# Four more projection units as seven products, and the solve's transfers on two queues

## The chip, the cores and the metric

The kernel runs on one core of a Trainium2 chip. The metric is device time in microseconds of one execution; lower is better. A profiled execution gives a trace beside it: every instruction with its engine and time, every DMA, and who waited for whom. The engines are TensorE (PE, its weight loads PEld), VectorE (DVE), ScalarE (ACT), GpSimd (POOL) and SyncE (SP, which only issues DMAs here).

## The reference

One pre-norm residual layer over 1024 tokens of width 1024. Of one normalised input, a projection of 8208 columns feeds two mixers that run side by side: dilated attention in three groups, and a gated DeltaNet with a short causal convolution. Both are gated, projected up, merged by sigmoid gates and projected out. Cut to what matters here:

```python
h = _rmsnorm(x, norm_w[layer])
proj = h @ w_in[layer]
dsa_qkv, dsa_z, gdn_qkv, gdn_z, gdn_b, gdn_a, gate_a, gate_b = _split_columns(proj)
o_a = _dilated_mixture(q_a, k_a, v_a)
y_a = (o_a * jax.nn.silu(dsa_z)) @ w_up_a[layer]
cqkv = jax.nn.silu(_causal_depthwise_conv(gdn_qkv, conv_w[layer]))     # 4 taps
o_b = _gated_delta_rule(gq, gk, gv, g, beta)
y_b = (_rmsnorm(o_b, gdn_norm_w[layer]) * jax.nn.silu(gdn_z)) @ w_up_b[layer]
merged = jax.nn.sigmoid(gate_a) * y_a + jax.nn.sigmoid(gate_b) * y_b
x = x + merged @ w_out[layer]
# in _gated_delta_rule, per head and chunk of 64 tokens:
a = (k_beta @ k.T) * decay_strict
t_inv = triangular_solve(eye + a, eye)
u = t_inv @ (vc * beta)
w = t_inv @ (k_beta * jnp.exp(G))
# then a scan over the 16 chunks with a state per head
```

The result is (1, 1024, 1024) in float32.

## The kernel before, in words

**Products.** Inputs are float32; each operand is split into a high and a low float16 part, and a product is three float16 matmuls (lines L184 to L186 in `mm3_steps`). The normalised input stays in SBUF as `h_hi` and `h_lo`. The projection is cut into units of 256 columns: 18 for attention, 6 for the convolution (`gdn`, for two half-batches of heads `hb` and the kinds query 0, key 1, value 2), 4 for the output gates `z`, 8 for the merge gates (`gate`). A unit is done in one of two ways:

- `Normal`: four blocks of 128 columns by 512 tokens, each over 8 slices of the width, three matmuls a slice: 32 steps (ticks) of three matmuls. The weights come in two loads and are split in two calls of `split` (lines L167 for ACT, then L84 for DVE, 1024 elements each).
- `Seven`: a 2x2 by 2x2 block product with seven products instead of eight (a Strassen form). 7 x 4 ticks of three matmuls. Sums of the input's blocks (`sums`) are made once; sums of the weights' blocks are made on DVE (L329), and seven blocks of 512 are split (L330 on ACT, L84 on DVE). `seven_products` uses the three PSUM banks `ps_mm` in turn, copies between them on ACT (L367), and hands out results in the order (column block, token half) = (0,0), (1,1), (1,0), (0,1); the second and third come with a `rest` from which DVE subtracts the bank.

**Order.** PE runs in the order in which the program is written. `feed` holds the units in a list; `feed.tick(n)` writes the next n ticks into PE's order, between the steps of attention, of the solve or of the scan, `feed.until(name)` writes ticks until that unit is done, and `feed.later(n, fn)` runs a step n ticks on. For the other engines `set_orders` at the program's end plans an order from costs; on the chip each engine works its order off strictly, and a semaphore holds it where an operand is not there.

**The place of the change** lies between the last attention set and the scan. For each half `hb`: `decay` makes `E` (tiles `gm`), `sumsq` turns the keys and sums squares (`kss`), `pairs` makes key products, and DVE multiplies them by `E` into `MT`. `keys_side` stores `MT`'s diagonal blocks to DRAM (`m_d`) in four DMAs; `solve` loads them back as `As`, 128 systems of 32x32, one a partition, and works 31 steps of two DVE instructions (`stmp`, `X`), then a last scaling, and stores `X` (`u_d`) and its negated transpose `T` (`t_d`). Four loads bring `u_d` back into `MT` (there called `U`), two bring `t_d` to `T1p`. `merge` joins the 32x32 blocks to 64x64: `left` on PE reads `T1p`, DVE makes `Y` of it, `right` on PE reads `Y` and `U`. Both solves run one behind the other on DVE, in shared buffers. `state_parts` then makes and stores `un_d` and `w_d` for the scan. The weight loads (`wstage`) are issued by POOL, as are the stores `un_d` and `a_d`; the rest here by SP.

**Convolution.** `conv_unit` takes each block from PSUM to `xc` (515 columns: three of the quarter before, then 512), scales the last tap on ACT into `ca`, and adds three taps on DVE (three instructions `ca<-xc,cw,ca`), then applies the SiLU. It needs the two token halves of a column block in order, since the second starts with the last three columns of the first.

Of the kernel before, what the change touches and what calls it, by code (L numbers as in the profile page):

```python
# [38 lines left out]
def gdn_unit(hb, what):  # L39
# [6 lines left out]
          + [U_GATE + i for i in (0, 1, 2, 6, 7)] + [U_Z + i for i in range(4)])  # L46
# [11 lines left out]
STATE_LAG = 12  # L58
# [20 lines left out]
def hybrid_block(ctx: ExitStack, tc: tile.TileContext, A):  # L79
# [916 lines left out]
    def conv_unit(hb, what, dst_of, then=None):  # L996

        def gen(w):
            for c in range(2):
# [3 lines left out]
                for hf in range(2):  # L1003
                    def take(p):
                        with tc.high_priority():
# [8 lines left out]
                            for j in (2, 1, 0):  # L1014
                                STT(a, xc[:, j:j + 512], cw[:, cidx, j:j + 1], a, ALU.mult, ALU.add)
                            parts = [(dst[:, 8 * hf:8 * hf + 8].rearrange("p c i -> p (c i)"), lambda x: x)]
                            if hb:

                                dv = dst[:, 8 * hf:8 * hf + 8].rearrange("p (t c) i -> p t c i", c=2)
                                parts = [(dv[:, :, b], lambda x, b=b: x.rearrange("p (t c i) -> p t c i", c=2, i=64)[:, :, 1 - b])  # L1020
                                         for b in range(2)]
                            if (hb, what) in SILU:
                                for d, of in parts:
                                    SC.activation(d, of(a), AF.Silu, scale=2.0)
                            else:
                                th = pre[0].tile([128, 512], F32, name="cth", tag="cth", bufs=2)
                                SC.activation(th, a, AF.Tanh)
                                for d, of in parts:
                                    STT(d, of(th), 1.0, of(a), ALU.add, ALU.mult)
# [6 lines left out]
        feed.add(("gdn", hb, what), Normal(A["w"][gdn_unit(hb, what)]), gen)  # L1036
# [145 lines left out]
    def decay(hb):  # L1182

        for t in range(8):
# [18 lines left out]
            feed.tick(2)  # L1203
# [23 lines left out]
    def sumsq(hb, src, dst, take=None):  # L1227

        for t0 in range(0, 8, 2):
# [11 lines left out]
            feed.tick(2)  # L1241
# [36 lines left out]
    def keys_side(hb):  # L1278
# [12 lines left out]
        for kb in range(4):  # L1291
            b = kb % 2
            nc.sync.dma_start(out=m_d[kb].rearrange("n j i -> j n i"),
                              in_=MT[hb][32 * kb:32 * kb + 32].rearrange("p t e q i -> p (t e q) i")[:, :, 32 * b:32 * b + 32])
# [13 lines left out]
    def solve(hb, m_d, bsc):  # L1308
# [24 lines left out]
        for kb in range(4):  # L1333
# [4 lines left out]
            nc.sync.dma_start(out=U[32 * kb:32 * kb + 32].rearrange("p t e q i -> p (t e q) i")[:, :, 32 * b:32 * b + 32],  # L1338
# [128 lines left out]
    gate_unit(5, gate_spill)  # L1467
# [52 lines left out]
    for i in (6, 7):  # L1520
        gate_unit(i, gate_spill)
# [851 lines left out]
```

## Time and profile before

| | |
|---|---|
| median of 3 runs | 1049.75 us (1048.6 to 1051.1) |
| profiled execution | 1048.82 us; its span in the trace 1047.0 us |
| PE busy | 1029.0 us, 98% |
| DVE busy | 885.7 us, 85% |
| ACT busy | 583.0 us, 56% |
| granted clock of TensorE | 0.998 |

Times in the trace count from the span's start. A group line gives the line of the code, the engine, what is written and read, count, busy time and mean length of one, and then the idle time of the engine just before it with what ended that wait. SPq rows are issues of DMAs, not their transfers.

### The profile page before, as it was taken

The page shows a single profiled execution, that of the slowest core. Times are in us where ns is not written, and L with a number is a line of the kernel's source. Part 1 is how long each engine was busy: PE and PEld are TensorE (multiplying, and loading weights), DVE is VectorE, ACT ScalarE, POOL GpSimd, SP SyncE. Part 2 cuts the span into 40 slices and gives each one's busy share as a digit, 9 for nine tenths or more (in the row PEclk, how much of TensorE's full clock was granted, in tenths as well). Part 3 has the DMA queues.
Part 4 walks back from the last instruction along what each step waited for, and adds up shares of the span by engine and source line. Part 5 has one row for each costly group of instructions (what it writes and reads, how often), then busy time and mean ns, then how long its engine had stood idle before and what let it go on. Part 6 is the DMA issues. An engine that isn't in the chain of part 4 may idle for free.

```text
span 1047.0 us, 24924 instructions
## 1 busy us (share of the span) xinstructions
PE 1029.0 (98%) x9962; PEld 632.9 (60%) x9962; DVE 885.7 (85%) x2052; ACT 583.0 (56%) x1322; POOL 56.1 (5%) x107
## 2 busy tenths in 40 slices
PE   6999999999999999999999999999999999999997
PEld 5995595775966855876655545545555555444444
DVE  6898988979979889989998897976588768899934
ACT  6455767777767766667756633344444345344523
POOL 0000000000000000010010000110100001000000
PEclk9999999999999999999999999999999999999999
DMA  8144531542624622470146357794874415743232
GB/s 284 64 129 114 138 112 62 152 112 78 186 84 116 165 91 74 118 201 28 43 161 183 113 134 202 258 278 150 266 254 152 142 62 176 288 124 117 67 115 81
DMA packets 99780, 148.53 MB, mean 142 GB/s; under 512 B 31168, under 2 KB 64704, under 8 KB 98512
## 3 DMA queue, kind: packets, MB, share of 16 engines
q1 hardware_dynamic: 69264, 84.64, 27.9%
q0 software_dynamic: 12320, 44.11, 13.4%
q10 hardware_dynamic: 18080, 18.20, 5.0%
q8 instruction: 78, 1.28, 0.5%
q14 instruction: 38, 0.31, 0.1%
HBM read 91.13 MB, written 36.90 MB: 122 GB/s over the span
## 4 chain that ended last, share of the span: by engine, by line
PE 84%; DVE 10%; ACT 2%; DMA 1%; issue 1%; SPq 0%; DVEq 0%; ACTq 0%
PE ps_mm L184 21%; PE ps_mm L186 20%; PE ps_mm L185 20%; PE ps_G L813 2%; PE ps_S L186 2%; PE ps_S L185 2%; PE ps_S L184 2%; DVE ca L84 1%; PE ps_S L790 1%; PE ps_S L792 1%; PE ps_G L185 1%; PE ps_G L186 1%; PE ps_G L184 1%; DVE sm L799 1%; DVE tl L87 1%
## 5 line engine op out<-in xcount | busy, mean ns | idle before, releaser
L186 PE MATMUL ps_mm<-h_hi,wlo 128*128 128x512 f16 (+1 forms) x504 | 189.3, 376 | 0.0
L184 PE MATMUL ps_mm<-h_hi,whi 128*128 128x512 f16 (+1 forms) x436 | 163.8, 376 | 0.0
L185 PE MATMUL ps_mm<-h_lo,whi 128*128 128x512 f16 (+1 forms) x436 | 163.5, 375 | 0.0
L186 PEld LDWEIGHTS <-wlo 128*128 128x128 f16 x748 | 73.2, 98 | 81.4
L184 PEld LDWEIGHTS <-whi 128*128 128x128 f16 x816 | 79.9, 98 | 65.7
L185 PEld LDWEIGHTS <-whi 128*128 128x128 f16 x816 | 79.9, 98 | 64.4
L803 ACT ACTIVATE sm<-sm,osb 128x128 f32<-128x128 f32 (+1 forms) x160 | 69.3, 434 | 34.9 <-DVE osb L799 33.3
L330 ACT ACTIVATE whi<-wstage 128x512 f16<-128x512 f32 x84 | 51.1, 626 | 30.0 <-DVE wstage L329 11.9
L799 DVE CUSTOM_DVE_ANT_0 sm<-ps_S,amask 128x128 f32<-128x128 f32 (+1 forms) x192 | 60.3, 345 | 6.6 <-PE ps_S L792 6.5
L87 DVE TENSOR_TENSOR tl<-ps_G,th 128x256 f16<-128x256 f32 (+1 forms) x96 | 51.7, 539 | 13.3 <-ACT th L818 13.0
L84 DVE SCALAR_TENSOR_TENSOR whi<-wstage,whi 128x512 f16<-128x512 f32 x84 | 57.2, 684 | 4.6 <-ACT whi L330 4.4
L329 DVE TENSOR_TENSOR wstage<-wstage 128x512 f32<-128x512 f32 x84 | 56.9, 685 | 0.8
L185 PE MATMUL ps_mm<-wlo,h_hi 128*128 128x256 f16 (+1 forms) x256 | 57.3, 246 | 0.0
L84 DVE SCALAR_TENSOR_TENSOR ca<-xc,cw,ca 128x512 f32<-128x512 f32 x72 | 53.7, 745 | 3.8 <-ACT ca L1013 3.3
L184 PE MATMUL ps_mm<-h_hi,wlo 128*128 128x512 f16 x136 | 51.6, 380 | 0.0
L185 PE MATMUL ps_mm<-h_lo,wlo 128*128 128x512 f16 x136 | 51.5, 379 | 0.0
L84 DVE SCALAR_TENSOR_TENSOR wlo<-wstage,whi 128x1024 f16<-128x1024 f32 x38 | 46.1, 1218 | 6.3 <-ACT whi L167 5.6
L818 ACT CAST th<-ps_G 128x256 f16<-128x256 f32 (+1 forms) x96 | 44.0, 458 | 12.5 <-PE ps_G L813 10.8
L813 PE MATMUL ps_G<-cons,sm 128*128 128x128 f32 x280 | 46.9, 274 | 1.3 <-ACT sm L803 1.2
L84 DVE SCALAR_TENSOR_TENSOR wlo<-wstage,wlo 128x512 f16<-128x512 f32 x63 | 42.4, 683 | 6.2 <-ACT wlo L330 6.2
L313 POOL DMA_DIRECT2D wstage<-in_w x42 | 22.2, 530 | 473.2 <-DVE whi L84 154.9
L184 PE MATMUL ps_mm<-whi,h_hi 128*128 128x256 f16 (+1 forms) x192 | 46.5, 256 | 0.0
(492 smaller groups left out, 2950.3 us busy)
## 6 DMA issues: line engine op xcount, KB each, us to landing
wstage<-in_w POOLq DMA_DIRECT2D x68, 512.0 KB, 4.5
og<-osb ACTq DMA_DIRECT2D x32, 132.0 KB, 2.2
og<-og SPq DMA_DIRECT2D x32, 132.0 KB, 2.4
sga<-gspa SPq DMA_DIRECT2D x8, 512.0 KB, 9.1
wstage<-in_w_up POOLq DMA_DIRECT2D x8, 512.0 KB, 5.3
sgb<-gspb SPq DMA_DIRECT2D x8, 512.0 KB, 4.2
wos<-in_w_out SPq DMA_DIRECT2D x8, 512.0 KB, 4.7
xr<-in_x SPq DMA_DIRECT2D x8, 512.0 KB, 4.1
```

Source lines behind the costliest of these rows:

```text
L84: (eng or V).scalar_tensor_tensor(out, in0, scalar, in1, op0=op0, op1=op1)
L87: (eng or V).tensor_tensor(out, in0, in1, op)
L184: PE.matmul(out, lhsT=wh(k), rhs=mh(k), start=first and i == 0, stop=False, skip_group_check=True)
L185: PE.matmul(out, lhsT=wh(k), rhs=ml(k), start=False, stop=False, skip_group_check=True)
L186: PE.matmul(out, lhsT=wl(k), rhs=mh(k), start=False, stop=last and i == len(ks) - 1, skip_group_check=True)
L313: nc.gpsimd.dma_start(out=st, in_=self.src[n])
L329: V.tensor_tensor(self.part[name], self.part[x], self.part[y], ALU.add)
L330: SC.activation(t[:, b, 0], self.part[name], AF.Copy, scale=W_SCALE)
L799: V.tensor_tensor_reduce(P[:, u, :128 * nk], psc[:, u * 256:u * 256 + 128 * nk], mask, -cexp, -NEG, ALU.add, ALU.min, accum_out=osb[:, 256 ...
L803: SC.activation(P[:, u, :128 * nk], P[:, u, :128 * nk], AF.Exp, bias=osb[:, 256 + hd:257 + hd], scale=-1.0, accum_out=osb[:, 260 + hd:261 ...
L813: PE.transpose(pt[:, c:c + 128], P[:, u, i * 128:i * 128 + 128], ident)
L818: SC.copy(th[:, :n], pt[:, :n])
```

## The change

Four more units become `Seven`: gates 3, 4 and 5 and the query unit of the second half, `gdn(1, 0)`. All eight gates are then of that kind.

For the query unit `conv_unit` gets a second generator. The results come in the order (0,0), (1,1), (1,0), (0,1), and the convolution needs (1,0) before (1,1): the `xc` of (1,1) is kept (`held`) and finished behind (1,0). The last three columns of a first half go to a small tile `edge`. The filter itself is the same code, moved to `filtered`.

Numbers of ticks change: in `decay` 2 becomes 1 for four of the eight blocks of each half, in `sumsq` 2 becomes 1 for the first half, and `STATE_LAG` 12 becomes 8. Gate 6 moves ahead of the `z` units, and the scan's end waits for the last `z` unit instead of gate 6. Of the four stores `m_d` two go to POOL's queue, and of the four loads of `u_d` two.

```diff
 SEVENS = ([att_unit(g, hs, w) for g in (1, 0) for hs in range(2) for w in range(3)]
-          + [U_GATE + i for i in (0, 1, 2, 6, 7)] + [U_Z + i for i in range(4)])
+          + [gdn_unit(hb, w) for hb, w in [(1, 0)]] + [U_GATE + i for i in (0, 1, 2, 3, 4, 5, 6, 7)] + [U_Z + i for i in range(4)])
-STATE_LAG = 12
+STATE_LAG = 8
@@ conv_unit
+        def gen7(w):
+            dst, edge, held = {}, {}, []
+
+            def shifted(c, hf, p, rest):
+                xc = pre[0].tile([128, 515], F32, name="xc", tag="xc", bufs=2)
+                if hf == 0:
+                    V.memset(xc[:, 0:3], 0.0)
+                if rest is None:
+                    SC.copy(xc[:, 3:515], p)
+                else:
+                    STT(xc[:, 3:515], p, -1.0, rest, ALU.mult, ALU.subtract)
+                if hf == 0:
+                    edge[c] = pre[0].tile([128, 4], F32, name="edge", tag="edge", bufs=2)
+                    V.tensor_copy(edge[c][:, 0:3], xc[:, 512:515])
+                return xc
+
+            def finish(c, hf, xc):
...
+                if hf:
+                    V.tensor_copy(xc[:, 0:3], edge[c][:, 0:3])
+                a = pre[0].tile([128, 512], F32, name="ca", tag="ca", bufs=2)
+                SC.activation(a, xc[:, 3:515], AF.Copy, scale=cw[:, cidx, 3:4])
+                filtered(c, hf, xc, a, dst[c], cidx)
...
+            def out(c, hf, p, rest):
+                with tc.high_priority():
+                    xc = shifted(c, hf, p, rest)
+                    if (c, hf) == (1, 1):
+                        held.append(xc)
+                        return
+                    finish(c, hf, xc)
+                    if (c, hf) == (1, 0):
+                        finish(1, 1, held[0])
+
+            yield from seven_products(w, out)
+
+        add_unit(("gdn", hb, what), gdn_unit(hb, what), gen, gen7)
@@ decay
-            feed.tick(2)
+            feed.tick(2 - (hb ^ (t > 3)))
@@ sumsq
-            feed.tick(2)
+            feed.tick(1 + hb)
@@ keys_side
-            nc.sync.dma_start(out=m_d[kb].rearrange("n j i -> j n i"),
+            (nc.sync, nc.gpsimd)[b].dma_start(out=m_d[kb].rearrange("n j i -> j n i"),
@@ solve
-            nc.sync.dma_start(out=U[32 * kb:32 * kb + 32].rearrange("p t e q i -> p (t e q) i")[:, :, 32 * b:32 * b + 32],
+            (nc.sync, nc.gpsimd)[kb // 2].dma_start(out=U[32 * kb:32 * kb + 32].rearrange("p t e q i -> p (t e q) i")[:, :, 32 * b:32 * b + 32],
@@ the list of units
-    gate_unit(5, gate_spill)
+    for i in (5, 6):
+        gate_unit(i, gate_spill)
...
-    for i in (6, 7):
-        gate_unit(i, gate_spill)
+    gate_unit(7, gate_spill)
@@ behind the scan
-    feed.until(("gate", 6))
+    feed.until(("z", "b", 1))
```

Since the other engines' orders are planned anew, the diff does not show what they do. At three places the order of instructions is shown before and after.

DVE, in the second half of the first solve's 31 steps (`stmp` and `X` are the solve; the sizes count the steps); before:

```order
L87 TENSOR_TENSOR stmp<-As,X 128x240
L87 TENSOR_TENSOR X<-X,stmp 128x20x12
L87 TENSOR_TENSOR stmp<-As,X 128x231
L87 TENSOR_TENSOR X<-X,stmp 128x21x11
L87 TENSOR_TENSOR stmp<-As,X 128x220
```

The same steps after (`whi<-wstage,whi` splits a block of a seven-product unit, `wstage<-wstage` sums two blocks):

```order
L87 TENSOR_TENSOR stmp<-As,X 128x240
L84 SCALAR_TENSOR_TENSOR whi<-wstage,whi 128x512
L87 TENSOR_TENSOR X<-X,stmp 128x20x12
L329 TENSOR_TENSOR wstage<-wstage 128x512
L87 TENSOR_TENSOR stmp<-As,X 128x231
L87 TENSOR_TENSOR X<-X,stmp 128x21x11
L84 SCALAR_TENSOR_TENSOR whi<-wstage,whi 128x512
L87 TENSOR_TENSOR stmp<-As,X 128x220
L329 TENSOR_TENSOR wstage<-wstage 128x512
```

The new units' weight work stands between the steps of the solve.

SP, from the first solve's results on (stores `u_d` and `t_d`, loads of `MT` and `T1p` from them, `As` for the second solve); before:

```order
L1329 DMA u_d_9062<-X 128x1024
L1330 DMA t_d_9063<-T_9060 128x1024
L1338 DMA MT_8581<-u_d_9062 32x32x32
L1336 DMA T1p<-t_d_9063 32x32x32 x2
L1338 DMA MT_8581<-u_d_9062 32x32x32
L1311 DMA As<-m_d_9433 128x1024
L1454 DMA rv_d<-rv 128x4x128
L1338 DMA MT_8581<-u_d_9062 32x32x32
L1395 DMA rvt<-rv_d 128x4x256
```

SP after:

```order
L1372 DMA u_d_9022<-X 128x1024
L1373 DMA t_d_9023<-T_9020 128x1024
L1497 DMA rv_d<-rv 128x4x128
L1381 DMA MT_8581<-u_d_9022 32x32x32
L1354 DMA As<-m_d_9386 128x1024
L1379 DMA T1p<-t_d_9023 32x32x32 x2
L1438 DMA rvt<-rv_d 128x4x256
L1381 DMA MT_8581<-u_d_9022 32x32x32
```

POOL after, with the other two loads of `MT`:

```order
L313 DMA wstage<-in_w 128x1024 x2
L1358 MEMSET X 128x1024
L1381 DMA MT_8581<-u_d_9022 32x32x32
L1359 MEMSET X 128x32
L1381 DMA MT_8581<-u_d_9022 32x32x32
```

`As` of the second solve moved ahead of `T1p`, and two loads of `MT` from SP to POOL, behind two weight loads.

DVE at the second merge (`Y` follows `left` and is read by `right`; `rq` is a sum for the queries); before:

```order
L1254 TENSOR_REDUCE rq<-ps_O 128x2x4
L84 SCALAR_TENSOR_TENSOR whi<-wstage,whi 128x512
L329 TENSOR_TENSOR wstage<-wstage 128x512
L84 SCALAR_TENSOR_TENSOR ca<-xc,cw,ca 128x512
L87 TENSOR_TENSOR Y<-ps_S,pack 32x512 x2
```

After:

```order
L84 SCALAR_TENSOR_TENSOR whi<-wstage,whi 128x512
L84 SCALAR_TENSOR_TENSOR ca<-xc,cw,ca 128x512
L84 SCALAR_TENSOR_TENSOR whi<-wstage,whi 128x512
L329 TENSOR_TENSOR wstage<-wstage 128x512
L1060 COPY xc<-edge 128x3 x2
L84 SCALAR_TENSOR_TENSOR ca<-xc,cw,ca 128x512 x2
L87 TENSOR_TENSOR Y<-ps_S,pack 32x512 x2
```

The convolution of the query unit's last results, with the copies from `edge`, now stands just ahead of `Y`.

More of the change, by code (lines that the diff above doesn't have):

```diff
@@ L996, in conv_unit, with filtered @@
     def conv_unit(hb, what, dst_of, then=None):
+        def filtered(c, hf, xc, a, dst, cidx):
+            for j in (2, 1, 0):
+                STT(a, xc[:, j:j + 512], cw[:, cidx, j:j + 1], a, ALU.mult, ALU.add)
+            parts = [(dst[:, 8 * hf:8 * hf + 8].rearrange("p c i -> p (c i)"), lambda x: x)]
+            if hb:
+                dv = dst[:, 8 * hf:8 * hf + 8].rearrange("p (t c) i -> p t c i", c=2)
+                parts = [(dv[:, :, b], lambda x, b=b: x.rearrange("p (t c i) -> p t c i", c=2, i=64)[:, :, 1 - b])
+                         for b in range(2)]
+            if (hb, what) in SILU:
+                for d, of in parts:
+                    SC.activation(d, of(a), AF.Silu, scale=2.0)
+            else:
+                th = pre[0].tile([128, 512], F32, name="cth", tag="cth", bufs=2)
+                SC.activation(th, a, AF.Tanh)
+                for d, of in parts:
+                    STT(d, of(th), 1.0, of(a), ALU.add, ALU.mult)
         def gen(w):
@@ L1013, in take @@
                             SC.activation(a, p, AF.Copy, scale=cw[:, cidx, 3:4])
[L1014 to L1029, printed above, removed]
+                            filtered(c, hf, xc, a, dst, cidx)
                         last.append(xc)
@@ L1034, in gen @@
                     yield from proj(w, c, hf, take)
-        feed.add(("gdn", hb, what), Normal(A["w"][gdn_unit(hb, what)]), gen)
+        def gen7(w):
[6 more added lines that the diff above has]
+                    SC.copy(xc[:, 3:515], p)
+                else:
+                    STT(xc[:, 3:515], p, -1.0, rest, ALU.mult, ALU.subtract)
[4 more added lines that the diff above has]
+            def finish(c, hf, xc):
+                cidx = 4 * what + 2 * hb + c
+                if c not in dst:
+                    dst[c] = dst_of(c)
+                if hf:
[3 more added lines that the diff above has]
+                filtered(c, hf, xc, a, dst[c], cidx)
+                if hf and then:
+                    then(c, dst[c])
+            def out(c, hf, p, rest):
[9 more added lines that the diff above has]
+        add_unit(("gdn", hb, what), gdn_unit(hb, what), gen, gen7)
     kT, pre = [], []
```

## The prediction

> **What bounds the kernel now.** I read the page first: busy time, then the chain that ended last.
>
> ```profile
> span 1047.0 us, 24924 instructions
> PE 1029.0 (98%) x9962; PEld 632.9 (60%) x9962; DVE 885.7 (85%) x2052; ACT 583.0 (56%) x1322; POOL 56.1 (5%) x107
> PE 84%; DVE 10%; ACT 2%; DMA 1%; issue 1%; SPq 0%; DVEq 0%; ACTq 0%
> ```
>
> TensorE (PE) is busy nearly throughout and carries 84% of the chain, so the time is the length of its stream plus its waits. Busy time overstates a pipelined engine, so next came the timeline, for the pace of the projections' matmuls (start, duration, instruction):
>
> ```profile
> 460.04 0.38 PE L186 MATMUL ps_mm<-h_hi,wlo 128*128 128x512 f16 x1
> ...
> 462.63 0.38 PE L186 MATMUL ps_mm<-h_hi,wlo 128*128 128x512 f16 x1
> ```
>
> Each lasts 0.38 us, but the second row starts twelve matmuls after the first: 2.59 / 12 = 0.216 us apiece. That is the price of a matmul that is taken out.
>
> Third, the engine beside PE. I cut the busy times by stretches where the change works: up to the end of the first solve, to the end of the second, to the last product that the second merge waits for, and to the scan. The columns are PE, its weight loads, VectorE (DVE), ScalarE (ACT), POOL, clock, DMA.
>
> ```profile
> 545.30:629.30 84.00, 82.97 (x664) 44.20 (x662) 75.14 (x151) 44.16 (x75) 5.72 (x12) 1.00 0.52 150
> 629.30:691.90 62.60, 61.97 (x771) 32.37 (x769) 54.63 (x112) 23.30 (x39) 8.86 (x15) 1.00 0.78 236
> 691.90:716.10 24.20, 24.20 (x293) 12.72 (x292) 16.59 (x27) 10.21 (x20) 1.64 (x3) 1.00 0.93 271
> 716.10:757.00 40.90, 40.90 (x737) 23.76 (x735) 20.86 (x33) 16.44 (x30) 7.53 (x13) 1.00 0.61 197
> ```
>
> PE has no wait worth naming here. DVE is idle for 84.00 - 75.14 = 8.9 us, then 8.0, then 7.6, and has 20 us free before the scan. The case turns on these idle times, because the change takes work from PE and gives work to DVE at this place.
>
> **PE's part.** A unit of 256 columns takes 4 blocks x 8 x 3 = 96 matmuls as plain products and 7 x 4 x 3 = 84 as seven. Four units change: 48 matmuls, 48 x 0.216 = 10.4 us. Three matmuls make a tick, so that is 16 ticks. The edited numbers take out 8 ticks ahead of the first `pairs`, 4 more ahead of the second, and 4 in `STATE_LAG`; the `until` behind the second conv gives 8 back. Counted along PE's order, the first `pairs` stands 24 matmuls earlier (5.2 us), the first merge 12 (2.6 us), the second merge and the scan 36 (7.8 us), the end 48. Their times now:
>
> ```profile
> 562.80 0.58 PE L1269 MATMUL ps_G<-kT 64*64 64x64 f32 x24
> 644.36 0.62 PE L1353 MATMUL ps_S<-T1p,MT 32*32 32x32 f32 x27
> 649.27 0.21 PE L1353 MATMUL ps_S<-T1p,MT 32*32 32x32 f32 x1
> 713.10 0.38 PE L1353 MATMUL ps_S<-T1p,MT 32*32 32x32 f32 x12
> 718.01 0.21 PE L1368 MATMUL ps_G<-MT,Y 32*32 32x32 f32 x1
> ```
>
> So, if nothing is late, the first merge's left half is due at 641.8 and its right half at 646.7, the second's left at 705.3 and right at 710.2.
>
> **What it costs beside PE.** The groups of the whole run (count, busy us, mean ns):
>
> ```profile
> L84 DVE SCALAR_TENSOR_TENSOR whi<-wstage,whi 128x512 f16<-128x512 f32 x84 | 57.2, 684 | 4.6 <-ACT whi L330 4.4
> L329 DVE TENSOR_TENSOR wstage<-wstage 128x512 f32<-128x512 f32 x84 | 56.9, 685 | 0.8
> L84 DVE SCALAR_TENSOR_TENSOR wlo<-wstage,whi 128x1024 f16<-128x1024 f32 x38 | 46.1, 1218 | 6.3 <-ACT whi L167 5.6 <-ACT qT L1213 0.5
> L84 DVE SCALAR_TENSOR_TENSOR wlo<-wstage,wlo 128x512 f16<-128x512 f32 x63 | 42.4, 683 | 6.2 <-ACT wlo L330 6.2
> L330 ACT ACTIVATE whi<-wstage 128x512 f16<-128x512 f32 x84 | 51.1, 626 | 30.0 <-DVE wstage L329 11.9 <-PE ps_mm L186 10.2 <-PE ps_mm L185 6.5
> L367 ACT COPY ps_mm<-ps_mm 128x512 f32<-128x512 f32 x42 | 24.1, 573 | 21.9 <-PE ps_mm L186 21.7
> L84 DVE SCALAR_TENSOR_TENSOR gst<-ps_mm,x 128x512 f32<-128x512 f32 x1 | 0.7, 681 | 0.0
> L84 DVE SCALAR_TENSOR_TENSOR rx<-ps_mm,x 128x512 f32<-128x512 f32 x24 | 19.3, 806 | 1.9 <-PE ps_mm L186 1.9
> ```
>
> On DVE a unit's weights cost 4 sums and 7 splits, 4 x 0.685 + 7 x 0.684 = 7.5 us, in place of 2 x 1.218 = 2.4. Its results add two subtractions from PSUM: 0.68 each for a gate; those of the query block are not in the trace, and I bound them by 0.68 and 0.81 and take 0.7, as they too are written in one piece. That is 5.1 + 1.4 = 6.5 us a unit, 26 us for four. The edge copies of three columns are some 0.2 us each. ACT gets three PSUM copies (1.7 us) and seven casts of 0.626 for two twice as long, some 4 us a unit; it is busy 44.16 of 84.00 and then 23.30 of 62.60, which hides them. DVE's queue moves on faster than the durations say:
>
> ```profile
> 586.84 0.69 DVE L84 SCALAR_TENSOR_TENSOR vT<-cth,ca 128x512 f32<-128x512 f32 x1
> 587.44 2.48 DVE L87 TENSOR_TENSOR As<-As,bsc 128x1024 f32<-128x1024 f32 x2
> ...
> 627.59 0.74 DVE L84 SCALAR_TENSOR_TENSOR ca<-xc,cw,ca 128x512 f32<-128x512 f32 x1
> 628.25 1.04 DVE L1326 TENSOR_SCALAR T<-X 128x1024 f32<-128x1024 f32 x1
> ...
> 642.12 1.22 DVE L87 TENSOR_TENSOR As<-As,bsc 128x1024 f32<-128x1024 f32 x1
> 645.61 1.41 DVE L87 TENSOR_TENSOR Y<-ps_S,pack 32x512 f32<-32x512 f32 x2 [2.27 <-PE ps_S L1353]
> ...
> 714.64 1.41 DVE L87 TENSOR_TENSOR Y<-ps_S,pack 32x512 f32<-32x512 f32 x2
> ```
>
> A 0.69 us row is followed after 0.60, a conv step after 0.66; I count 0.61, 0.66, and 1.14 for a split of 1024. Counting DVE's order between the same marks: up to the first `T` there are 21 more short rows (8 sums, 11 splits, 2 subtractions) and 3 more conv steps, and 4 fewer long splits: 12.8 + 2.0 - 4.6 = +10.2 us. From there to the second `T`: 19 more short rows, 1 conv step and 3 long splits fewer: +7.5 us. From there to the second merge's `Y`: within 0.5 us of none. The other 8 us fall behind it, where 20 us are free. DVE works its order off strictly, so the last of these four rows' counterpart ends no sooner than 545.3 + 75.1 + 10.2 + 54.6 + 7.5 + 16.6 = 709.3, plus whatever DVE idles. The right half of the second merge reads it and is due at 710.2. The spare is 0.9 us.
>
> **How much DVE will idle** is the one large unknown: between nothing and all it idled in the first two stretches, 16.9 us. I build it from the waits. First stretch, 2.5 of 8.9: rows in it that wait for products of PE's order (the eight decay blocks, the conv's blocks) now have weight splits in front; what stays is the wait for the second half of `pairs`, some 1.5 us, and a us of short ones. So the first `T` ends at 545.3 + 75.1 + 10.2 + 2.5 = 633.1, 3.8 us later than now. Second stretch, 3.5 of 8.0: the way out and back over DRAM does not shrink.
>
> ```profile
> 576.48 0.46 SPq L1311 DMA_DIRECT2D As<-m_d  x1
> ...
> 629.33 0.34 SPq L1330 DMA_DIRECT2D t_d<-T  x1
> 632.32 0.93 SPq L1336 DMA_DIRECT2D T1p<-t_d  x2
> 633.90 1.17 SPq L1311 DMA_DIRECT2D As<-m_d  x1
> ...
> 691.91 0.33 SPq L1330 DMA_DIRECT2D t_d<-T  x1
> 696.26 1.54 SPq L1336 DMA_DIRECT2D T1p<-t_d  x2
> DMA to landing us min/median/max: 2.8/4.8/7.5
> DMA to landing us min/median/max: 4.8/4.8/4.9
> ```
>
> `T` ends at 629.3 and the loads of `T1p` go out 3.0 us later, landing 2.8 to 7.5 us after issue (the last rows: `T1p`, then `As`). The next `As` uses the room of `T`, so it too waits for that store; now it is issued ahead of `T1p`. With 4.8 us to land it is there about 8 us behind `T`, and DVE has 6.6 us of other rows meanwhile: 1.5 us of idling, and 2 for products, against 2.3 on the `Y` row alone now. The second `T` ends at 633.1 + 54.6 + 7.5 + 3.5 = 698.7, and `Y` at 698.7 + 16.6 = 715.3.
>
> **First merge.** `T1p` is there some 7 to 9 us behind 633.1, at 640 to 642, where 641.8 is due: of a margin of 8 us now, 0 to 1.5 is left. The blocks of `U` that the right half reads come half from SP, behind the 512 KB of `rvt`, and half from POOL. I take 1 us of wait here, which shifts the rest and is inside the second wait, not beside it.
>
> **Second merge.** The left half waits for `T1p` at 698.7 + 3.0 (a store, 4.3 the last time) + 5 to 7.5, 707 to 711 for 705.3. The right half starts when `Y` is done: 715.5 for 710.2, a wait of 5.3 us in all. In the same 10 us lies the query block's end: its kept quarter holds one `xc` buffer, the last result waits for the conv of the one before (subtraction and three steps, 2.7 us), and the next gate's second product needs that PSUM bank after 12 matmuls, 2.6 us. With DVE that late PE waits there too, but for the same DVE rows: no second charge.
>
> **Two queues.** Four stores of `MT` stand on SP now, four blocks of `U` come back over it; half of each goes to POOL.
>
> ```profile
> 569.12 4.66 SPq L1293 DMA_DIRECT2D m_d<-MT  x4
> L1437 POOL DMA_DIRECT2D un_d<-uw x16: 631/631/659, 666.7 to 737.7; - x16
> ```
>
> SP spends 4.66 us on four; two on each would end 2.3 us sooner (POOL's nearest row is 0.63 us each). I book 0: `As` is issued at 576.48 and lands at 581.3, but DVE takes it at 587.44: 6 us are covered by DVE's own order, and both move up with `pairs`. If POOL stands behind a weight load whose buffer DVE has not freed, those 6 us are the cover. [...]
>
> **The rest.** Gate 6 now runs ahead of the scan and the z units follow it; its two loads on POOL, 11 DVE rows and four spills move with it. From the second merge to the scan PE keeps 126 projection matmuls, DVE gets +5 us on 20.86 of 40.90: covered; if DVE were still 5 us behind, it would catch up there. The last 12 matmuls saved lie behind the scan, where PE runs without waits.
>
> **Sum**, against the profiled execution (1048.8 us, 1.8 beyond its span): 1048.8 - 10.4 + 5.3 = 1043.7. The median shown, 1049.75, stands 0.9 above it: 1044.7.
>
> **Rivals.** (1) DVE closes its gaps: idle under 1 us, no wait, 1049.75 - 10.4 = 1039.4. For it: in the stretch from 545.3 it is already 89% busy with far less to choose from. Against it: the store and load behind each `T` cannot be filled. (2) DVE's lateness eats the saving: idle 9.2 to 13.4 us gives waits of 8.3 to 12.5 us and 1047.65 to 1051.85, no change. (3) The second solve becomes the bound and the kernel slower. The place is the second merge, the price one us of PE per us of DVE idling beyond 0.9; it decides from an idle of 13.4 us on (10.4 + 2.1 + 0.9). If all 16.9 us stay, the wait is 16.0 and the time 1055.3. For it: those gaps were waits for PE, whose order is no denser. Against: the split rows that fill them need no product of PE. (4) The clock falls in a long wait:
>
> ```profile
> 1040.00:1047.00 7.00, 0.37 (x4) 0.09 (x1) 3.15 (x13) 2.38 (x5) 0.00 (x0) 0.71 0.41 150
> ```
>
> PE does 0.37 us in the last 7 and its granted clock there is 0.71; every other stretch above has 1.00, with no wait over 1 us. A wait of 5 us in one piece could be followed by as long at that mean pace, 5 x (1/0.71 - 1) = 2 us: 1046.7. I think the wait comes in pieces (left half, right half, the bank), with matmuls between. [...]
>
> **Chances.** Forecast, waits of 3 to 8.3 us, with or without the clock: 0.46. Rival 1 and waits under 3 us: 0.25. Rival 2: 0.17. Rival 3: 0.12. About 0.2% (2.1 us) is what a measurement can tell from no change here; faster by that is 0.71, within it 0.17, slower 0.12. The range runs from no wait, 1039.4, to a wait of 10.5 us, 1049.9.
>
> **What would show it.** Right: 48 fewer 128x512 matmuls; DVE over 95% busy from 545 to 700; the first `T` ending near 633 and the second near 699; PE waits at the lines of the merges, ended by DVE `Y` or the load of `T1p`, 4 to 6 us in sum; none in the scan. Wrong: the second `T` before 694 (then rival 1) or after 706 (rival 3); waits at the projection lines for PSUM banks elsewhere; a granted clock under 1.00 between 640 and 720.

## The result, and the profile after

The changed kernel takes 1056.01 us in the median (at the least 1050.97), the kernel before 1049.75 us: a ratio of 1.005, with a 95% interval of 1.0037 to 1.0063. It is slower by half a per cent, where 1044.7 us and a range up to 1049.9 were forecast. Two of its runs, which took over 1500 us, are left out of the comparison. Its profiled execution took 1054.07 us.

The lines of its page that answer to those shown of before:

```profile
span 1052.3 us, 24915 instructions
PE 1025.2 (97%) x9914; PEld 630.3 (60%) x9914; DVE 902.9 (86%) x2098; ACT 595.9 (57%) x1352; POOL 62.5 (6%) x115
PE 75%; DVE 14%; DMA 5%; ACT 3%; issue 2%; SPq 0%; POOL 0%; DVEq 0%; ACTq 0%; POOLq 0%
```

PE issues 9914 matmuls for 9962: the 48 are gone. But its share of the chain fell from 84% to 75%, and DMA carries 5% of it, against 1% before. The chain now passes through transfers.

The busy times by stretches, cut at the marks of this execution (end of the first `T`, of the second, the last product ahead of the second merge's right half, the start of the scan), and then three short ones. The last three columns are the granted clock, the DMA share and GB/s:

```profile
545.30:633.59 88.29, 87.31 (x684) 46.16 (x683) 83.48 (x178) 50.73 (x91) 8.74 (x15) 1.00 0.46 131
633.59:697.89 64.30, 62.74 (x828) 32.60 (x826) 60.09 (x127) 29.43 (x52) 10.88 (x18) 1.00 0.82 250
697.89:719.97 22.08, 17.84 (x189) 9.58 (x188) 19.55 (x36) 9.19 (x19) 3.81 (x6) 0.85 0.92 261
719.97:767.42 47.45, 44.43 (x743) 24.85 (x742) 26.91 (x46) 21.49 (x41) 7.52 (x13) 0.96 0.63 205
712.00:718.80 6.80, 6.80 (x77) 3.99 (x76) 4.30 (x8) 1.15 (x2) 0.53 (x1) 0.50 0.91 270
759.80:763.20 3.40, 3.40 (x9) 1.21 (x8) 2.42 (x8) 0.15 (x1) 0.00 (x0) 0.50 0.61 198
701.00:711.00 10.00, 6.43 (x32) 3.01 (x30) 10.00 (x21) 5.88 (x12) 0.80 (x3) 1.00 1.01 255
```

Up to the second `T` PE is nearly as busy as before, at full clock. Then it is not: two stretches, 6.8 and 3.4 us long, run at half clock. Each stands right behind a wait in PE's timeline; the brackets hold the idle time and what ended it:

```profile
707.05 0.38 PE L186 MATMUL ps_mm<-h_hi,whi 128*128 128x512 f16 x1
711.56 0.86 PE L1396 MATMUL ps_S<-T1p,MT 32*32 32x32 f32 x16 [4.13 <-DMA T1p<-t_d]
...
755.27 0.38 PE L186 MATMUL ps_mm<-h_hi,wlo 128*128 128x512 f16 x1
758.67 0.66 PE L1293 MATMUL ps_O<-cons,qT 128*128 128x128 f32 x4 [3.02 <-DVE rq L1297]
```

The first is the second merge, waiting for `T1p`. The second is the last of the query sums ahead of the scan, waiting for DVE. What kept each, in the timelines of SP and of DVE:

```profile
697.92 0.33 SPq L1373 DMA_DIRECT2D t_d<-T  x1
699.06 0.83 SPq L1580 DMA_DIRECT2D sga<-gspa  x2
699.98 0.40 SPq L1381 DMA_DIRECT2D MT<-u_d  x1
701.22 7.54 SPq L1379 DMA_DIRECT2D T1p<-t_d  x2
...
755.99 0.69 DVE L329 TENSOR_TENSOR wstage<-wstage 128x512 f32<-128x512 f32 x1 [3.19 <-DMA wstage<-in_w]
756.60 0.69 DVE L84 SCALAR_TENSOR_TENSOR whi<-wstage,whi 128x512 f16<-128x512 f32 x1
757.32 0.69 DVE L329 TENSOR_TENSOR wstage<-wstage 128x512 f32<-128x512 f32 x1
757.93 0.69 DVE L1297 TENSOR_REDUCE rq<-ps_O 128x8 f32<-128x512 f32 x1
```

Between the store of `T` and the loads of `T1p`, SP sends two loads of `sga`, 512 KB each, the gates' spilled halves that the last projections first read at 892 us, 190 us later. The two loads of `T1p` then take 7.54 us to issue, and land 13.5 and 13.9 us behind `T`. Before the change the same `sga` loads went out behind `T1p`:

```profile
696.26 1.54 SPq L1336 DMA_DIRECT2D T1p<-t_d  x2
697.86 2.81 SPq L1338 DMA_DIRECT2D MT<-u_d  x1
...
705.05 1.36 SPq L1537 DMA_DIRECT2D sga<-gspa  x2
```

In the second wait DVE's `rq` stands behind a sum of the next gate's weights, whose load was 10.2 us on its way (issued at 745.66, landed at 755.90).

Laid beside the due times of the prediction's count (us; lateness is measured minus due):

| place | before | due | measured | late | grown since the row above |
|---|---|---|---|---|---|
| first `pairs` | 562.80 | 557.6 | 559.04 | 1.4 | 1.4 |
| first merge, left | 644.36 | 641.8 | 644.00 | 2.2 | 0.8 |
| second merge, left | 713.10 | 705.3 | 711.56 | 6.3 | 4.1 |
| scan, first product | 759.84 | 752.0 | 767.42 | 15.4 | 9.1 |
| end of the span | 1047.0 | 1036.6 | 1052.3 | 15.7 | 0.3 |

Of the 15.7 us at the end, 13.2 arose between the first merge's left half and the scan; 1.4 were there at the first `pairs` already. At half clock the projections' matmuls start 0.43 us apart (714.08 and 714.51), not 0.216, so half of the 6.8 us and half of the 3.4 us are lost, 5.1 us; the second wait is another 3.0: 8.1 of the 9.1 us between the second merge and the scan.

### The profile page after: what moved, and what is told of

The parts are those of the page before. It is cut to its first block, busy times and chain, and to the rows that moved or that the text cites. A ratio compares the mean times of both kernels' runs of the same rounds, so it can differ in the third digit from the quotient of the medians.

```text
span 1052.3 us, 24915 instructions
## 1 busy us (share of the span) xinstructions
PE 1025.2 (97%) x9914; PEld 630.3 (60%) x9914; DVE 902.9 (86%) x2098; ACT 595.9 (57%) x1352; POOL 62.5 (6%) x115
## 3 DMA queue, kind: packets, MB, share of 16 engines
q0 software_dynamic: 12704, 45.16, 14.3%
## 4 chain that ended last, share of the span: by engine, by line
PE 75%; DVE 14%; DMA 5%; ACT 3%; issue 2%; SPq 0%; POOL 0%; DVEq 0%; ACTq 0%; POOLq 0%
PE ps_mm L184 18%; PE ps_mm L185 17%; PE ps_mm L186 17%; DVE ca L84 2%; PE ps_G L813 2%; PE ps_S L184 2%; PE ps_S L185 2%; PE ps_S L186 2%; DMA wstage<-in_w 2%; DMA T1p<-t_d 1%; PE ps_S L790 1%; PE ps_S L792 1%; PE ps_G L184 1%; PE ps_G L186 1%; PE ps_G L185 1%
## 5 line engine op out<-in xcount | busy, mean ns | idle before, releaser
L186 PE MATMUL ps_mm<-h_hi,wlo 128*128 128x512 f16 (+1 forms) x408 | 153.0, 375 | 0.0
L184 PE MATMUL ps_mm<-h_hi,whi 128*128 128x512 f16 (+1 forms) x324 | 121.8, 376 | 0.0
L185 PE MATMUL ps_mm<-h_lo,whi 128*128 128x512 f16 (+1 forms) x324 | 121.7, 376 | 0.0
L184 PEld LDWEIGHTS <-whi 128*128 128x128 f16 x752 | 73.9, 98 | 59.3 <-issue 1.3
L185 PEld LDWEIGHTS <-whi 128*128 128x128 f16 x752 | 73.9, 98 | 59.1 <-issue 2.5
L330 ACT ACTIVATE whi<-wstage 128x512 f16<-128x512 f32 x100 | 61.1, 627 | 31.6 <-PE ps_mm L186 14.6
L84 DVE SCALAR_TENSOR_TENSOR whi<-wstage,whi 128x512 f16<-128x512 f32 x100 | 68.1, 686 | 6.9 <-ACT whi L330 6.6
L329 DVE TENSOR_TENSOR wstage<-wstage 128x512 f32<-128x512 f32 x100 | 68.2, 688 | 3.9 <-DMA wstage<-in_w 3.2
L184 PE MATMUL ps_mm<-h_hi,wlo 128*128 128x512 f16 x168 | 63.9, 380 | 0.0
L185 PE MATMUL ps_mm<-h_lo,wlo 128*128 128x512 f16 x168 | 63.7, 379 | 0.0
L87 DVE TENSOR_TENSOR tl<-ps_G,th 128x256 f16<-128x256 f32 (+1 forms) x96 | 52.1, 543 | 13.2 <-ACT th L818 12.9
L186 PEld LDWEIGHTS <-whi 128*128 128x128 f16 x336 | 33.2, 99 | 40.8 <-issue 1.9
L330 ACT ACTIVATE wlo<-wstage 128x512 f16<-128x512 f32 x75 | 46.4, 628 | 17.0 <-DVE wstage L329 9.6
```

Of the source, the lines that this page charges most:

```text
L84: (eng or V).scalar_tensor_tensor(out, in0, scalar, in1, op0=op0, op1=op1)
L87: (eng or V).tensor_tensor(out, in0, in1, op)
L184: PE.matmul(out, lhsT=wh(k), rhs=mh(k), start=first and i == 0, stop=False, skip_group_check=True)
L185: PE.matmul(out, lhsT=wh(k), rhs=ml(k), start=False, stop=False, skip_group_check=True)
L186: PE.matmul(out, lhsT=wl(k), rhs=mh(k), start=False, stop=last and i == len(ks) - 1, skip_group_check=True)
L329: V.tensor_tensor(self.part[name], self.part[x], self.part[y], ALU.add)
```

## The experiments

Theory A: the second merge was moved ahead of its data, by `STATE_LAG` and the other ticks. Theory C: the loads of `sga` in front of `T1p` are the cause. Theory E: the half clock is a price of its own for standing still in one piece. Each run was timed beside the kernel before on one chip; the ratio to it is given with its 95% interval. Differences between two kernels are taken from their medians; by the ratios they come out up to 1.6 us otherwise. Every edit also lets the orders of the other engines be planned anew. By the traces, 2 of DVE's 2098 instructions stand elsewhere in the run with late `sga` loads than in the changed kernel, both behind the scan's start. In the two runs with idle matmuls at least 29 and 45 do, against the same kernel without them, with one queue in the fastest version 47, and with `STATE_LAG` 16 (without the cap told of below) 215. So only the first of these edits tests one thing alone.

**The second merge later, first attempt.**

```
-STATE_LAG = 8
+STATE_LAG = 16
...
-    feed.tick(OB_LAG)
+    feed.tick(OB_LAG, ("z", "b", 1))
...
-            feed.tick(4)          # beside the last transposes
+            feed.tick(4, ("z", "b", 1))
...
-    feed.tick(1)
+    feed.tick(1, ("z", "b", 1))
```

> STATE_LAG 8 becomes 16, all else as changed: 24 more projection matmuls (5.2 us) stand ahead of the second merge, and the same work fewer behind it. Theory A (the solve was moved ahead of its data): in the changed kernel PE waited 4.3 us for T1p at 711.56 and then ran 6.83 us at half clock, 3.4 us lost, so 7.7 us in all. With 5.2 us more work the load is there in time: both are gone. If the 3.18 us wait ahead of the scan (with 3.41 us at half clock, 4.9 us in all) is a consequence of the late second merge, it goes too: 1056.0 - 7.7 - 4.9 = 1043.4. If it has its own cause (a weight load that lands at 755.90), it stays: 1048.3. Rival B (DVE's later T and the loads in front of T1p just follow PE): the wait stays at 3 us or more and the time at 1054 to 1056.

Measured: 1071.89 us, 1.021 (1.0193 to 1.0227). A miss, but not by either theory. In the profile the second merge has no long wait and no half clock, and the scan began at 764.16 with 24 more matmuls done. The loss is behind the scan. The second argument of `tick`, which the expectation does not mention, is a cap that I had added so that the later ticks would not run into the next projections before their buffers exist. I set it at the last z unit; in the changed kernel those ticks run on into gate 7.

```profile
865.11 0.30 PE L1806 MATMUL ps_G<-cons,ob 128*128 128x128 f32 x1 [4.49 <-DVE ob L87]
...
901.58 0.58 PE L184 MATMUL ps_mm<-h_hi,wlo 128*128 128x512 f16 x1 [12.34 <-DVE gst L84]
```

Without the 60 matmuls that stood beside the transposes, PE waits for DVE there, 4.5 and 12.3 us, and runs 10.2 and 13.7 us at half clock. The same cap spoils the two runs that share it:

> Both edits: STATE_LAG 16 and the four sga loads late. If both waits come from these two (Theories A and C), none over 1 us is left, the granted clock is 1.00 from 545 to 1040, and the time is 1056.0 - 7.7 - 4.9 = 1043.4 or up to 1 us less. If the wait ahead of the scan has another cause (the order of gate 6's weights on DVE), it stays: 1048.3.

Measured: 1071.45 us, 1.0206 (1.0184 to 1.0227), with the same two waits (4.49 and 12.14 us). And all 16 ticks given back, with gate 6, queues and `sga` as changed:

```
-STATE_LAG = 8
+STATE_LAG = 12
...
-            feed.tick(2 - (hb ^ (t > 3)))
+            feed.tick(2)
...
-            feed.tick(1 + hb)
+            feed.tick(2)
```

> All 16 ticks given back (STATE_LAG 12, decay and sumsq at 2 ticks as before), so the solve stands behind as many projection matmuls as before the change; the four units as seven products, gate 6 ahead of the z units and the two queues stay. Theory A: the first T ends some 3 to 4 us later than before in time but its merge is due 2.6 us later than in the changed kernel and the second 7.8 us: no wait over 1.5 us, clock 1.00, 1049.75 - 10.4 + 1 to 3 = 1040.4 to 1042.4. Rival D (the sevens cost DVE more than PE gains wherever the solve stands): DVE's later rows hold PE at the second merge all the same, and the time is 1048 or more.

Measured: 1094.16 us, 1.0401 (1.0373 to 1.0428), with 20.6 us of such a wait in the last gate and 9.15 us at the first merge, at 656.16, behind a first `T` that ended at 641.27. The time decides nothing on the ticks, since the cap is in it. But the cap acts behind the scan and cannot have made the wait at the first merge. There `T` came 7.7 us later than in the changed kernel and the loads of `T1p` landed 14.9 and 15.1 us behind it, not 10.4 and 11.1. Giving the ticks back moved the solve's data too, so it did not bring them in time, and that speaks against Theory A at this merge. What the three show is that matmuls taken from one place are missed at another: the ticks are a fixed stock, 48 matmuls smaller since the change.

**The `sga` loads late.** The first result of the z units is written into one column of the tile ahead of the load, so that the load cannot start before it:

```
+        if dt < SIG_AHEAD:
+            GP.tensor_copy(sig["a", dt][:, 0:1], osp["a", 0][:, 0, 0:1])
         for br in "ab":
             nc.sync.dma_start(out=sig[br, dt], in_=gsp[br, dt])
```

> The four 512 KB loads of sga, two of which stand on SP between t_d and T1p and two at 745 us, wait for a result of the first z block and so go out behind the scan's start. Ticks as changed. Theory A (the position of the merge alone): T1p still comes some 12 us behind T (before: 10 to 12.2), at 709 to 710 where PE runs dry at 707.4: a wait of 2 to 2.5 us instead of 4.3; time 1050 to 1054. Theory C (the loads in front of T1p are the cause): T1p's loads, which took 3.07 and 4.42 us to issue and landed 13.9 us behind T, land at 706 to 708, the wait is under 1 us with no half clock: 7 us less. If the same loads at 745 made the weight load slow (10.2 us to landing against 6.5 for the one before it), the wait ahead of the scan goes too: 1044 to 1046; if not, 1049.

Measured: 1048.64 us, 0.9991 (0.998 to 1.0001): 7.4 us below the changed kernel. SP at the second merge:

```profile
702.43 0.33 SPq L1373 DMA_DIRECT2D t_d<-T  x1
703.54 0.32 SPq L1381 DMA_DIRECT2D MT<-u_d  x1
707.39 0.93 SPq L1379 DMA_DIRECT2D T1p<-t_d  x2
```

`T1p` takes 0.93 us to issue and lands 9.4 and 10.3 us behind `T`, not 13.5 and 13.9. The waits of the merge are 0.63 and 1.48 us, the clock stays at 1.00 there, and the wait ahead of the scan is gone too. This speaks for C; the landing is as late as A gave it (9 to 12 us behind `T`). `T` itself came 4.5 us later than in the changed kernel, after PE had stood still and run at half clock at 470 and at the first merge (see the last section), so by the clock `T1p` was no earlier; what changed is its distance from `T`. That distance parts all versions of the changed kernel: with `sga` in front (six of them) the later load of `T1p` landed 13.4 to 17.2 us behind the second `T`, with late `sga` (six) 8.3 to 11.0. The time is 2.6 us above the 1044 to 1046 expected where both waits go; those two stretches at half clock, 3.4 us each, had not been expected.

The control, the same edit in the kernel before:

> The kernel before the change, with the four sga loads held back in the same way. There T1p's loads were issued ahead of sga's and PE had no wait worth naming at the merges. Theory C says that the late loads gain only where sga stands in front of T1p: within 0.2% of before, 1048 to 1051. Rival I (512 KB loads in this stretch slow every transfer, the late position is simply better): 1046 or less.

Measured: 1049.49 us, 0.9988 (0.9977 to 0.9998), within 0.2%. Late loads gain where they stood in front of `T1p`, and next to nothing where they did not.

**The second merge later, without the cap.** The same `STATE_LAG` 16; the last ticks are capped at gate 7, which they now just reach.

> STATE_LAG 16 again, now with the matmuls of gate 7 left beside the last transposes as in the changed kernel; the first attempt had capped the ticks there at the last z unit and so took 60 matmuls away from that place. The sga loads stand as in the change. Theory A: the second merge comes 5.2 us later, T1p is there, no half clock at 712 (the capped run showed none there, and its scan began 3.3 us earlier with 24 matmuls more behind it, 8.5 us in all): 1056.0 - 8.5 = 1047.5. If gate 7, now ending with the last tick, runs out beside the transposes: up to 1 us more. Rival J (the 22 us of the capped runs came from the later merge, not from the cap): 1065 or more.

Measured: 1045.62 us, 0.9966 (0.9949 to 0.9982): one number of the change put from 8 to 16, and it is 10.4 us faster than the changed kernel and faster than the kernel before. The `sga` loads still stand in front, and `T1p` landed 14.6 and 15.4 us behind `T`, later than in the changed kernel; but now it is due later still:

```profile
714.29 1.20 PE L1396 MATMUL ps_S<-T1p,MT 32*32 32x32 f32 x64
...
697.89:719.97 22.08, 21.48 (x300) 11.56 (x297) 21.16 (x39) 12.63 (x26) 3.83 (x6) 1.00 1.04 270
719.97:764.01 44.04, 42.07 (x686) 23.41 (x674) 27.52 (x46) 21.77 (x40) 8.67 (x15) 1.00 0.68 214
```

No idle time ahead of `left`, 1.36 us ahead of a later part of the merge (at 721.44), a clock of 1.00, and only 0.6 us of idling from there to the scan, with gate 6 where the change put it. The wait ahead of the scan went for a reason that Theory A does not hold: with eight more ticks ahead of the merge the weight load left POOL at 736.55, before the two stores of `E` (`a_d`, 512 KB each) and the `sga` loads, and landed at 744.82. In the changed kernel it left at 745.66 among them (`a_d` at 745.06 and 746.86, `sga` at 745.11 and 745.55) and landed at 755.90; in the run with late `sga` it left at 744.45 among the stores alone and landed at 751.20. So the second wait is a meeting of transfers; the ticks moved one of them and the late `sga` took another out. A and C remove the same waits by two ends; their gains do not add.

**The clock.** Twenty matmuls that nothing reads, ahead of the second merge's left half, in the changed kernel:

```
             py = bank("S", 2)
+            for _ in range(20 if hb and not g else 0):
+                PE.matmul(py, lhsT=h_hi[:, 0, 0:128], rhs=h_hi[:, 0, 0:512], start=True, stop=True)
```

> The changed kernel with 20 idle 128x512 matmuls (20 x 0.216 = 4.3 us; their result is overwritten) right ahead of the second merge's left half, where PE waited 4.30 us. They stand on PE but nothing depends on them. Theory E (the drop of the clock is a price of its own, paid because PE stood still in one piece): the merge starts at the same 711.6, the stretch at half clock from 712.0 to 718.8 is gone, and the time falls by half of it, 3.4 us, to 1052.6; if the wait ahead of the scan was only its consequence, it falls further, to 1048. Rival F (the clock at that place falls for another reason, or what follows waits for DVE anyway): 1056 or, since the idle matmuls only add work, up to 1060.

Measured: 1052.55 us, 1.0013 (1.0 to 1.0026), 3.5 us less with more work. PE's timeline and the stretch behind it:

```profile
705.83 4.48 PE L1393 MATMUL ps_S<-h_hi 128*128 128x512 f16 x20
710.24 0.24 PE L1398 MATMUL ps_S<-T1p,MT 32*32 32x32 f32 x2
711.25 0.44 PE L1398 MATMUL ps_S<-T1p,MT 32*32 32x32 f32 x16 [0.77 <-DMA T1p<-t_d]
...
711.00:720.00 9.00, 7.64 (x216) 4.82 (x217) 6.54 (x10) 3.75 (x8) 0.54 (x1) 1.00 0.85 283
```

The half clock is gone, as Theory E has it, and the gain is the 3.4 us that it gave. What the half clock costs can be read in the changed kernel itself, where PE is busy for all 6.80 us at 0.50. That the whole gain is the clock's is not shown: DVE's order changed with the edit, `T` came 2.9 us earlier, and the left half started 1.3 us earlier, though `T1p` was no nearer to `T` (14.3 and 16.2 us behind it). The profiled execution was also the fastest of the 12, at 1047.92. The wait ahead of the scan stayed in part, at full clock; 1.32 of the 3.02 us are left, and the rest went with the lateness:

```profile
754.21 0.66 PE L1293 MATMUL ps_O<-cons,qT 128*128 128x128 f32 x4 [1.32 <-DVE rq L1297]
```

**Both ends, and the first merge.** Late `sga` loads, and ticks shifted without changing their sum up to the scan:

```
-UW_LAG = (12, (10, 4), 6)
+UW_LAG = (8, (10, 2), 6)
-STATE_LAG = 8
+STATE_LAG = 10
-M_LAG = 12
+M_LAG = 16
```

> The late sga loads, and the ticks shifted without changing their sum: M_LAG 12 to 16 and 4 fewer between the two parts of the first state (the first merge 12 matmuls, 2.6 us, later), STATE_LAG 8 to 10 and 2 fewer behind the second merge (the second merge 6 matmuls, 1.3 us, later); the scan and the end stay where they were. In the run with late loads alone PE waited 1.16 + 0.93 us in the first merge, with 3.4 us at half clock, and 0.3 + 0.79 + 1.64 us in the second. Theory A and C together: the first merge's wait and its clock drop go (2.1 + 1.7 us), the second's falls by about 1: 1048.6 - 4.8 = 1043.8. Rival (DVE is the clock of this stretch, so that a later merge only makes T's successors later): within 1 us of 1048.6.

Measured: 1047.28 us, 0.9966 (0.9953 to 0.998). The first merge's wait and its half clock are gone as expected. The second's grew: `T` came at 702.53, `T1p` in two pieces, 0.72 and 3.21 us of idling, and 6.8 us at half clock. To fill that:

> The run with late loads and the shift by 10, plus 16 idle matmuls (16 x 0.216 = 3.5 us) right ahead of the second merge's left half, where it waited 0.88 + 3.37 us and ran 6.83 us at half clock. Theory E: the wait is filled, the clock stays at 1.00, and only the 3.4 us of the clock are gained: 1043.9. Rival F: no gain, 1047 or more.

Measured: 1048.86 us, 0.9989 (0.9973 to 1.0004): a miss. In its profile (an execution of 1046.49 us) `T` came at 699.06, 3.5 us earlier than in the run without the filling, so `T1p` was there in time, and the 16 matmuls only cost their own time (the row below). `T` came earlier because the edit changed DVE's order: three steps of the convolution (`ca`) and a subtraction (`xc`) that had stood ahead of `T` stand behind it here. So the run does not price the filling. It shows instead that DVE's order in front of `T` is worth some 3.5 us of `T`'s time.

```profile
707.99 3.62 PE L1393 MATMUL ps_S<-h_hi 128*128 128x512 f16 x16
```

With the second merge 24 matmuls later than in the change (`STATE_LAG` 16, the 2 ticks behind the merge given back, the last ticks capped at gate 7):

> The late sga loads, the first merge 12 matmuls later (M_LAG 16, 4 ticks fewer between the parts of the first state), and STATE_LAG 16: the second merge 24 matmuls later than in the changed kernel, 18 later than in the run with the shift by 10. There PE still waited 0.88 + 3.37 us in the second merge and ran 6.83 us at half clock. With 3.9 us more work ahead of it 0.4 us of wait and no half clock are left: 1047.3 - 3.9 - 3.4 = 1040.0, 0.9% below before. Rival (DVE is late for what comes behind: the right half, the scan's sums): 1043 to 1045.

Measured: 1045.03 us, 0.9953 (0.9937 to 0.997). It has the lowest median, and is called the fastest version below: 11 us under the changed kernel and 0.47% under the kernel before, but 5 us above the 1040.0 expected. From the run with `STATE_LAG` 16 alone (0.9966) the intervals do not tell it apart. No clock falls in it ahead of the last microseconds, and no merge waits for `T1p`:

```profile
649.14 1.20 PE L1396 MATMUL ps_S<-T1p,MT 32*32 32x32 f32 x64
716.78 1.20 PE L1396 MATMUL ps_S<-T1p,MT 32*32 32x32 f32 x64
```

The gap to 1040.0 is not one wait. In its profile PE idles longer than before by 0.9 us in the first 460 us, which the change does not touch, 0.9 from 460 to 548, 0.8 from 548 to 640 and 1.7 from 640 to 770; the longest single wait in these stretches behind 460 is 1.80 us, at 471.77.

**The queues.** The changed kernel with all those transfers on SP:

```
-            (nc.sync, nc.gpsimd)[b].dma_start(
+            nc.sync.dma_start(
...
-            (nc.sync, nc.gpsimd)[kb // 2].dma_start(
+            nc.sync.dma_start(
```

> The changed kernel with the stores of MT and the loads of U all on SP again, as before the change. Theory (two queues worth nothing on the path): 1055 to 1057. Rival G (POOL's share gets the first merge's data in earlier): on SP the two more MT loads stand around T1p in the queue and each costs about 0.5 us of issue, the first merge's wait of 1.66 us grows to 2.5 to 3 us and the second from 4.30 to about 5: 1057 to 1060. Rival H (POOL's stores, 0.80 us each, and its loads compete with T1p): the waits shrink by 1 us and the time is 1052 to 1054.

Measured: 1057.06 us, 1.0064 (1.0046 to 1.0083). By the median it is one us slower, inside the interval, but its profile, of an execution of 1061.26 us, shows 7.61 us of idling at the first merge, and less at the second. Waits that follow each other may cover for each other there, so the price was taken again in the fastest version, which has none:

> The fastest version so far (late sga loads, M_LAG 16, STATE_LAG 16; 1045.0 us) with the stores of MT and the loads of U all on SP, as before the change. It prices the two queues where no merge has a long wait. In its trace with two queues the first T1p landed 11 and 12 us behind T, PE waited under 0.6 us there and the clock stayed at 1.00. Theory (two queues worth nothing on the path): 1045 within 1.5 us. Rival G (POOL takes loads out of T1p's way): in the changed kernel on one queue T1p's two loads were issued 7.7 us behind T instead of 3.2 and 3.7, and PE waited 8.5 us with 10.2 us at half clock; here the merge is 2.6 us later, so 4 to 6 us of wait and 3.4 of clock: 1050 to 1055.

Measured: 1050.73 us, 1.0016 (1.0002 to 1.0029), 5.7 us more than with two queues; rival G. SP at the first merge, with two queues and with one:

```profile
638.20 0.53 SPq L1381 DMA_DIRECT2D MT<-u_d  x1
639.33 0.32 SPq L1354 DMA_DIRECT2D As<-m_d  x1
639.70 1.05 SPq L1379 DMA_DIRECT2D T1p<-t_d  x2
```

```profile
641.03 0.46 SPq L1381 DMA_DIRECT2D MT<-u_d  x1
641.58 0.51 SPq L1354 DMA_DIRECT2D As<-m_d  x1
642.15 3.40 SPq L1379 DMA_DIRECT2D T1p<-t_d  x2
...
650.87 0.24 PE L1396 MATMUL ps_S<-T1p,MT 32*32 32x32 f32 x2 [2.81 <-DMA T1p<-t_d]
651.85 1.31 PE L1396 MATMUL ps_S<-T1p,MT 32*32 32x32 f32 x62 [0.73 <-DMA T1p<-t_d]
```

On one queue `T` is 1.6 us later and the loads of `T1p` take 3.40 us to issue, not 1.05, with another load of `rvt` ahead of them in SP's order. They land 12.8 and 13.8 us behind `T`, not 11.0 and 12.0; PE idles 3.5 us, runs 3.4 us at half clock, and waits again for the operands behind the merge. How much of it is the order on SP, how much POOL's own issue, and how much DVE's order, which changed with the edit (the second `T` came 5.8 us later), was not separated.

## Why the prediction was wrong, by its steps

**PE's part** was right: 48 matmuls fewer, and the positions in PE's order as counted.

**DVE's part** was right at its marks: the first `T` ended at 633.59 for 633.1, the second at 697.89 for 698.7. The sums and splits between the solve's steps cost what their rows said. But part of this is luck. By the stretches above, DVE was busy 8.3 and 5.5 us longer than before, where 10.2 and 7.5 were counted, and idle 4.8 and 4.2 us, where 2.5 and 3.5 were taken; the errors cancel. `Y` at 715.2 for 715.3 is luck altogether. DVE had done the rows ahead of it at 712.07 and then waited for PE's left half:

```profile
713.79 1.41 DVE L87 TENSOR_TENSOR Y<-ps_S,pack 32x512 f32<-32x512 f32 x2 [1.72 <-PE ps_S L1396]
```

**First merge**: 1 us was booked; PE idled 0.84 and 0.50 us for the two loads of `T1p`. They landed 10.4 and 11.1 us behind `T`, where 7 to 9 were taken.

**Second merge**, the step that failed first. The 5.3 us that were booked are a wait of the right half for `Y`. There was none: `Y` was done at 715.2, and PE reached the right half at 719.97 without a wait. PE waited for `T1p`, 4.13 us ahead of the left half. For that load "a store, 4.3 the last time" and "5 to 7.5" gave 707 to 711; it landed at 711.43 and 711.84, 13.5 and 13.9 us behind `T`, where it had been 10.2 and 12.2 before the change. I had read SP's order at the first way back over DRAM only and carried the old durations to the second, where the order has two 512 KB loads ahead of `T1p` and the DMA engines are full (a share of 1.01 from 701 to 711). So the sum, 5.3 us, was near the 4.13 by luck, since the wait was another one. And it was taken to be all that the lateness costs.

**The clock**, rival 4, was priced at 2 us and set aside with "I think the wait comes in pieces". It came in one, since the left half is the first thing to read `T1p`. The price was 3.4 us, half of 6.8 us in which PE was never idle, and 1.7 more at the second wait. A granted clock under 1.00 between 640 and 720, named as a sign of being wrong, is what the profile shows. The two stretches at half clock last 6.8 and 3.4 us. A shorter wait stood ahead of one, too: the 1.96 us at 470 in the run with late `sga` loads were followed by 3.4 us at half clock (the last section).

**The rest** failed: "if DVE were still 5 us behind, it would catch up there". DVE had the time, 26.91 us busy of 47.45; but it works in order, and a weight load in front of `rq` held it for 3.19 us. Lateness at the second merge did not fade by the scan, it grew there by 3.0 us of wait and 1.7 of clock. I had counted DVE's rows and not the loads that they wait for. The runs speak for two causes: the meeting with `a_d` and `sga`, without which the wait is gone, and the lateness, without most of which it is 1.32 us. The place of gate 6 by itself was not tried: with gate 6 behind the z units again, their results come before the buffers for them exist.

**Two queues** at 0 cannot be told from right in the changed kernel, where one queue took 1057.06 us for 1056.01. In the fastest version two queues were worth 5.7 us, DVE's changed order included: "two on each would end 2.3 us sooner" looked at the stores, and there the gain is on the loads. There the issue of `T1p` took 3.40 us on one queue and 1.05 on two, and it stood on the path.

**The rivals.** The outcome is rival 3's side with another mechanism: that rival wanted DVE to idle 13.4 us or more, but it idled 9.0 in the two stretches, and the second `T` came when the forecast said. Against the profiled execution the forecast was 1043.7; of the 10.4 us from there to 1054.07 the clock explains 5.1 and the wait ahead of the scan 3.0; the other 2.3 are not explained, but 1.4 us of lateness stood at the first `pairs` already. The median of after stands 1.9 us above its profile, that of before 0.9.

## What to carry over

Where an engine's stream is the time, a shorter stream is only a gain if everything that it reads is as much earlier; count the margin of each transfer at its own place in its queue, and look there for loads that are not urgent. Price a wait with what follows it: 2 to 4 us of standing still cost another 1.7 to 3.4 us of clock here, and the work that came late then met other transfers. When work that filled gaps is removed, say which gap it filled last: a cap that took the matmuls from beside the transposes cost 26 us (1071.89 against 1045.62). And where a plan is made anew with each edit, compare the orders before a difference in time is put down to the edit: filling a wait moved `T` by 2.9 and 3.5 us here.

## What had not been expected of the hardware

Of PE's waits of about 2 us in these runs some were followed by a lower clock, and others were not. In the run with late `sga` loads the softmax sum at 470, outside the change, idled PE for 1.96 us, and two stretches at half clock stand in that run:

```profile
470.12 0.71 PE L813 MATMUL ps_G<-cons,sm 128*128 128x128 f32 x2 [1.96 <-ACT sm L803]
647.04 0.24 PE L1396 MATMUL ps_S<-T1p,MT 32*32 32x32 f32 x2 [1.00 <-DMA T1p<-t_d]
648.05 1.15 PE L1396 MATMUL ps_S<-T1p,MT 32*32 32x32 f32 x52 [0.77 <-DMA T1p<-t_d]
...
471.20:474.70 3.50, 3.50 (x12) 1.59 (x10) 2.18 (x11) 2.89 (x10) 0.00 (x0) 0.51 0.35 135
648.70:652.20 3.50, 3.50 (x43) 2.28 (x36) 2.23 (x5) 2.11 (x2) 0.00 (x0) 0.51 1.05 295
```

The second stretch stands behind two waits of 1.00 and 0.77 us with two small products between them. In the changed kernel the clock fell 0.42 us behind the end of the wait of 4.13 us (at 711.98, for 6.8 us) and 1.09 us behind the end of the one of 3.02 us (at 759.76, for 3.4 us).

Two other single waits, of 1.80 and 2.18 us, were not followed by half clock: in the fastest version, behind the first, which ended at 471.77, the clock is 1.00 up to 476, and in the changed kernel on one queue, behind the second, which ended at 766.36, the projections' matmuls start 0.21 to 0.22 us apart up to 768. So the length of the wait alone does not tell whether the clock falls; what does, was not shown. Nor is it explained how long the half clock then lasts: 3.4 and 6.8 us in the changed kernel, 10.2 and 13.7 us in the first run with the cap.
